# Splitting the MLP weights of a hybrid decoder layer by two loads

## Chip, cores and metric

The kernel runs on one core of one Trainium2 chip. The metric is the device time of one execution in microseconds (us). The engines are TensorE (PE), VectorE (DVE), ScalarE (ACT), GpSimd (POOL) and SyncE (SP); SP, ACT and POOL can issue loads and stores, which the DMA engines carry out.

## The reference

One layer of a decoder with 512 tokens and 1024 features in float32. After a mixing part (a linear recurrence beside an attention) the layer has an MLP, which is what the change touches:

```python
    D_FF = 4 * D_MODEL                      # 4096
    x = x + merged @ w_out[l]
    h2 = rmsnorm(x, norm_mlp_g[l])
    x = x + jnp.square(jax.nn.relu(h2 @ w_mlp_up[l])) @ w_mlp_down[l]
    h3 = rmsnorm(x, norm_ple_g[l])
    x = x + jax.nn.sigmoid(h3 @ w_ple_gate[l]) * (p[l] @ w_ple[l])
```

## The kernel before

Every matrix product is made in three passes. Each operand is split into a high part, rounded to the type float32r, and a low part, the rest; `prod` (L116) issues high by high, high by low and low by high for each slice of 128 rows of the contraction, all into one PSUM bank (L119, L120, L121). In the MLP's products the weights are the stationary operand, so that L119 and L120 use the weights' high part and L121 the low part.

The weights come from DRAM in "halves" of 128 partitions by 1024 elements, 512 KB each. `halves` (L70 to L101) lists all of them in the order of their use: those of the mixing part first, then for each of the two halves h of the 4096 hidden features 16 halves `up{h}_*`, for h = 0 two halves `ple`, and 16 halves `dn{h}_*`; last the gate `pg`. The MLP has 64 halves, 32 of up and 32 of dn. A half of the MLP gives PE 24 matmuls of 128x512.

`next_half` (L104) hands out the half that is ready and writes down the work for the next one: `w_half` (L63) has the raw tile loaded on SP's queue (`load_raw`, L46 to L49), and `split` (L51 to L53) makes the high part on ACT as a copy that rounds (L52) and the low part on DVE as raw minus high (L53). The pool `wp` (L39) has three buffers for each of the tags raw, whi and wlo, so a tile can be written again when the half three places earlier is done with it.

The order of the instructions on each engine is not written by hand: the tile framework places them when the kernel is built, by a reckoned time line, and puts in the waits. Each engine's queue, and the queue of loads on SP, ACT and POOL, is then worked off in that fixed order.

In the MLP (L540 to L586) each half of up goes into one PSUM bank of the pool pq (four banks), and ACT takes it out with Relu (L546) and Square (L547); `split` rounds it into the tile ah on ACT and puts the rest in al on DVE. Two halves of dn make one bank, which DVE multiplies by the row scale (L580) and adds to the residual (L581). In the second round the residual is also split for the next product (L583), squared and turned (L584 to L586). Between up and dn of the first round PE makes the small product ple (L554 to L568).

Of the kernel before, what the change touches and what calls it, by code (L numbers as in the profile page):

```python
# [11 lines left out]
AF = mybir.ActivationFunctionType  # L12
ALU = mybir.AluOpType
# [18 lines left out]
def hybrid_layer(ctx, tc, xT, pT, vecs, gfin, gates, w_in, w_bl, w_ba, w_out,  # L32
                 w_up, w_dn, w_pg, w_ple, out):
    nc = tc.nc
    sc, ve, pe, gp, sy = nc.scalar, nc.vector, nc.tensor, nc.gpsimd, nc.sync
# [6 lines left out]
    def f32(ap):  # L42
        return ap.bitcast(F32)


    def load_raw(src, name):  # L46
        raw = wp.tile([P, 1024], F32, tag="raw", name="raw_" + name)
        sy.dma_start(raw, src)
        return raw  # L49

    def split(hi, lo, src):  # L51
        sc.copy(hi, src)  # L52
        ve.tensor_tensor(lo, src, f32(hi), op=ALU.subtract)  # L53
# [5 lines left out]
    def w_tiles(name):  # L59
        return (wp.tile([P, 1024], F32R, tag="whi", name="whi_" + name),  # L60
                wp.tile([P, 1024], F32R, tag="wlo", name="wlo_" + name))

    def w_half(src, name, kt):  # L63
        raw = load_raw(src, name)
        hi, lo = w_tiles(name)
        split(hi, lo, raw)
        return tuple(t.rearrange("p (k n) -> p k n", k=kt) for t in (hi, lo))


# [34 lines left out]
    def next_half(name):  # L104
        n, cur = state["ready"]
        assert n == name, (n, name)
        state["i"] += 1
        if state["i"] < len(halves):
            c = halves[state["i"]]
            state["ready"] = (c[0], w_half(c[1], c[0], c[2]))  # L110
        return cur
# [615 lines left out]
```

## Time and profile before

| | us |
|---|---|
| median of 3 runs | 945.73 |
| lowest and highest | 943.81, 948.19 |
| profiled execution, whole | 946.11 |
| profiled execution, span of its trace | 944.0 |
| PE busy in the span | 929.5 |
| DVE busy | 542.4 |
| ACT busy | 471.3 |
| POOL busy | 67.9 |

The profile is of one execution. The span runs from its first to its last recorded instruction; 2.1 us of the execution lie around it. PE's matmuls are pipelined, and each shows some 0.39 us where the next one starts 0.23 us later; the pace is read from the starts. Where a group shows idle time, the name behind the arrow is what ended it. The granted clock is that of PE as a share of its full speed (2.4 GHz).

### The profile page before, as it was taken

What the parts mean: (1) busy time and instruction counts of PE and PEld (TensorE: products, weight loads), DVE (VectorE), ACT (ScalarE), POOL (GpSimd) and SP (SyncE); (2) the same over time, 40 slices, a digit from 0 to 9 for tenths busy, and PEclk for the clock granted to TensorE, in tenths of its full rate; (3) what the DMA queues carried; (4) which work ended last, traced back from release to release, by engine and by line L of the source; (5) the groups of instructions that cost most, each with busy time, mean ns of one, the idle gap of its engine ahead of it and who ended that gap; (6) DMA issues with size and microseconds to landing.
All of it is one profiled execution on the core that took longest, in us unless ns stands there. A gap on an engine that the chain in (4) does not pass through costs nothing.

```text
span 944.0 us, 12123 instructions
## 1 busy us (share of the span) xinstructions
PE 929.5 (98%) x4634; PEld 790.9 (84%) x4634; DVE 542.4 (57%) x818; ACT 471.3 (50%) x751; POOL 67.9 (7%) x147
## 2 busy tenths in 40 slices
PE   8999999999999999999999999999999999999996
PEld 7988888888888888888888888888888888888896
DVE  6796947688998986534655433333333333344476
ACT  6567676667776765412334444541214554333443
POOL 0010000133233332000000000000000000000000
PEclk9999999999999999999999999999999999999998
DMA  6241222211222222432232223323223223222312
GB/s 220 95 134 67 90 90 85 95 68 67 68 68 68 67 68 68 173 111 95 90 109 92 90 90 104 119 90 101 100 90 108 94 89 107 94 90 90 112 45 90
DMA packets 25401, 89.42 MB, mean 95 GB/s; under 512 B 2944, under 2 KB 3200, under 8 KB 25088
## 3 DMA queue, kind: packets, MB, share of 16 engines
q1 hardware_dynamic: 24768, 87.61, 27.5%
q10 hardware_dynamic: 576, 1.05, 0.3%
q8 instruction: 36, 0.59, 0.3%
q14 instruction: 21, 0.17, 0.1%
HBM read 86.55 MB, written 2.10 MB: 94 GB/s over the span
## 4 chain that ended last, share of the span: by engine, by line
PE 95%; ACT 2%; DVE 1%; DMA 1%; issue 1%; SPq 0%; ACTq 0%
PE ps_up L119 6%; PE dn L121 6%; PE ps_up L121 6%; PE dn L119 6%; PE dn L120 6%; PE ps_up L120 6%; PE t L445 2%; PE pgt L120 2%; PE pgt L121 2%; PE pgt L119 2%; PE ps_gl L121 2%; PE ps_k L121 2%; PE ps_q L119 2%; PE ps_ga L121 2%; PE ps_q L120 2%; PE ps_k L119 2%
## 5 line engine op out<-in xcount | busy, mean ns | idle before, releaser
L119 PE MATMUL dn<-ah,whi_dn 128*128 128x512 f32 x256 | 100.2, 391 | 0.0
L119 PE MATMUL ps_up<-h,whi_up 128*128 128x512 f32 x256 | 99.9, 390 | 0.0
L121 PE MATMUL ps_up<-h,wlo_up 128*128 128x512 f32 x256 | 99.7, 390 | 0.0
L121 PE MATMUL dn<-ah,wlo_dn 128*128 128x512 f32 x256 | 99.7, 389 | 0.0
L120 PE MATMUL ps_up<-h,whi_up 128*128 128x512 f32 x256 | 99.6, 389 | 0.0
L120 PE MATMUL dn<-al,whi_dn 128*128 128x512 f32 x256 | 99.6, 389 | 0.0
L52 ACT CAST whi_dn<-raw_dn 128x1024 fp32r<-128x1024 f32 x32 | 33.6, 1053 | 108.3 <-PE dn L120 82.9
L53 DVE TENSOR_TENSOR wlo_up<-raw_up,whi_up 128x1024 fp32r<-128x1024 f32 x32 | 39.2, 1224 | 73.4 <-ACT whi_up L52 73.4
L52 ACT CAST whi_up<-raw_up 128x1024 fp32r<-128x1024 f32 x32 | 33.7, 1054 | 91.3 <-PE ps_up L120 62.9
L53 DVE TENSOR_TENSOR wlo_dn<-raw_dn,whi_dn 128x1024 fp32r<-128x1024 f32 x32 | 39.0, 1222 | 67.6 <-ACT whi_dn L52 67.6
L432 DVE TENSOR_TENSOR_SCAN pr<-r,zero 128x128 f32<-128x128 f32 (+1 forms) x64 | 54.1, 845 | 10.7 <-POOL r L155 10.2
L121 PEld LDWEIGHTS dn<-ah,wlo_dn 128*128 128x128 f32 x256 | 48.1, 188 | 10.1
L121 PEld LDWEIGHTS ps_up<-h,wlo_up 128*128 128x128 f32 x256 | 48.1, 188 | 10.0
L120 PEld LDWEIGHTS ps_up<-h,whi_up 128*128 128x128 f32 x256 | 48.1, 188 | 10.0
L120 PEld LDWEIGHTS dn<-al,whi_dn 128*128 128x128 f32 x256 | 48.1, 188 | 9.8
L119 PEld LDWEIGHTS ps_up<-h,whi_up 128*128 128x128 f32 x256 | 48.1, 188 | 9.8
L119 PEld LDWEIGHTS dn<-ah,whi_dn 128*128 128x128 f32 x256 | 48.1, 188 | 9.7
L155 POOL TENSOR_SCALAR_AFFINE_SELECT r<-r 128x128 f32<-128x128 f32 x64 | 29.8, 466 | 192.6 <-ACT r L428 190.2
L428 ACT ACTIVATE r<-z 128x128 f32<-128x128 f32 (+1 forms) x64 | 28.5, 445 | 27.7 <-PE z L424 27.0
L580 DVE TENSOR_TENSOR d<-dn,sumsq 128x512 f32<-128x512 f32 x16 | 11.1, 692 | 52.1 <-PE dn L121 52.1
L155 POOL TENSOR_SCALAR_AFFINE_SELECT s<-s 128x128 f32<-128x128 f32 x64 | 33.6, 525 | 5.1 <-ACT s L430 3.3
L434 DVE TENSOR_TENSOR s<-s,pr 128x127 f32<-128x127 f32 (+1 forms) x64 | 31.8, 498 | 3.6
(282 smaller groups left out, 2424.0 us busy)
## 6 DMA issues: line engine op xcount, KB each, us to landing
raw_up<-in_w_up_dram SPq DMA_DIRECT2D x32, 512.0 KB, 3.4
raw_dn<-in_w_dn_dram SPq DMA_DIRECT2D x32, 512.0 KB, 3.5
raw_u<-in_w_in_dram SPq DMA_DIRECT2D x16, 512.0 KB, 3.6
raw_qk<-in_w_in_dram SPq DMA_DIRECT2D x16, 512.0 KB, 3.5
raw_gl<-in_w_in_dram SPq DMA_DIRECT2D x8, 512.0 KB, 3.4
raw_ga<-in_w_in_dram SPq DMA_DIRECT2D x8, 512.0 KB, 3.4
raw_bl<-in_w_bl_dram SPq DMA_DIRECT2D x8, 512.0 KB, 3.4
raw_ba<-in_w_ba_dram SPq DMA_DIRECT2D x8, 512.0 KB, 3.4
```

The lines of the kernel that those rows point to most:

```text
L52: sc.copy(hi, src)
L53: ve.tensor_tensor(lo, src, f32(hi), op=ALU.subtract)
L119: pe.matmul(ps, lh, rh, start=(first and i == 0), stop=False)
L120: pe.matmul(ps, lh, rl, start=False, stop=False)
L121: pe.matmul(ps, ll, rh, start=False, stop=(last and i == n - 1))
L155: gp.affine_select(block, block, pattern=[[-1, P]], compare_op=ALU.is_gt, fill=fill, base=0, channel_multiplier=1)
L428: sc.activation(r[:, 0:w], z[:, 0:w], AF.Sigmoid, scale=-0.125)
L432: ve.tensor_tensor_scan(pr[:, 0:w][:, ::-1], r[:, 0:w][:, ::-1], zero.broadcast_to([P, w]), 1.0, op0=ALU.mult, op1=ALU.add)
L434: ve.tensor_tensor(s[:, 0:w - 1], s[:, 0:w - 1], pr[:, 1:w], op=ALU.mult)
L445: turned[kbs[0]] = pe.transpose(pt[:, o:o + P], att[qb][:, kb * P:(kb + 1) * P], ident)
L580: ve.tensor_tensor(t, ps, rs2, op=ALU.mult)
```

## The change

For the halves of up and dn, the raw tile and `split` go away. A load issued on POOL's queue brings the weights straight into the high part's tile, whose type is float32r, so that the load converts. ACT writes the negated high part into the low part's tile. A second load of the same weights, also on POOL's queue, adds to what stands in that tile. All other halves stay as they were.

```diff
     def w_half(src, name, kt):
-        raw = load_raw(src, name)
         hi, lo = w_tiles(name)
-        split(hi, lo, raw)
+        if name.startswith(("up", "dn")):
+
+            gp.dma_start(hi, src)
+            sc.activation(lo, f32(hi), AF.Copy, scale=-1.0)
+            gp.dma_start(lo, src, accum_op=ALU.add)
+        else:
+            split(hi, lo, load_raw(src, name))
         return tuple(t.rearrange("p (k n) -> p k n", k=kt) for t in (hi, lo))
```

## Rows read from the trace of the kernel before

**Rows 1.** The page's first part: busy us, share of the span, instructions of each engine.
```profile
span 944.0 us, 12123 instructions
PE 929.5 (98%) x4634; PEld 790.9 (84%) x4634; DVE 542.4 (57%) x818; ACT 471.3 (50%) x751; POOL 67.9 (7%) x147
```

**Rows 2.** Windows after attention: length, busy us (instructions), granted clock, DMA share, GB/s.
```profile
core 0: us, PE busy (x) PEld busy (x) DVE busy (x) ACT busy (x) POOL busy (x), PEclk, DMA share, GB/s
384.00:438.00 54.00, 54.00 (x240) 44.74 (x239) 23.21 (x29) 16.31 (x21) 0.00 (x0) 1.00 0.39 137
438.00:523.00 85.00, 85.00 (x377) 70.41 (x376) 47.37 (x60) 28.79 (x37) 0.00 (x0) 1.00 0.29 98
523.40:893.00 369.60, 369.60 (x1674) 307.18 (x1673) 138.53 (x156) 148.23 (x201) 0.00 (x0) 1.00 0.29 99
893.00:944.00 51.00, 42.42 (x355) 42.21 (x353) 34.66 (x117) 21.21 (x56) 0.00 (x0) 0.95 0.18 63
```

**Rows 3.** Timeline of dn, first round: start us, us, instruction, [idle before, its end].
```profile
639.76 1.05 ACT L52 CAST whi_dn<-raw_dn 128x1024 fp32r<-128x1024 f32 x1 [4.38 <-PE dn L120]
639.79 0.39 PE L119 MATMUL dn<-ah,whi_dn 128*128 128x512 f32 x1
640.24 0.39 PE L121 MATMUL dn<-ah,wlo_dn 128*128 128x512 f32 x1
...
645.20 1.05 ACT L52 CAST whi_dn<-raw_dn 128x1024 fp32r<-128x1024 f32 x1 [4.38 <-PE dn L120]
...
650.64 1.05 ACT L52 CAST whi_dn<-raw_dn 128x1024 fp32r<-128x1024 f32 x1 [4.39 <-PE dn L120]
650.67 0.39 PE L119 MATMUL dn<-ah,whi_dn 128*128 128x512 f32 x1
651.12 0.39 PE L121 MATMUL dn<-ah,wlo_dn 128*128 128x512 f32 x1
```

**Rows 4.** Loads of up (512 KB) and L508 (two of 1024 KB): issue ns, landing.
```profile
L48 SPq DMA_DIRECT2D raw_up<-in_w_up_dram x32: 327/328/328, 498.7 to 767.2; - x32
DMA to landing us min/median/max: 3.0/3.4/4.0
...
L508 SPq DMA_DIRECT2D x<-in_xT_dram x2: 328/377/426, 391.8 to 392.2; - x2
DMA to landing us min/median/max: 5.0/6.0/7.1
```

**Rows 5.** Groups of instructions: busy us, mean ns of one, idle before.
```profile
L52 ACT CAST whi_dn<-raw_dn 128x1024 fp32r<-128x1024 f32 x32 | 33.6, 1053 | 108.3 <-PE dn L120 82.9 <-issue 15.1 <-PE ps_up L120 10.3
L53 DVE TENSOR_TENSOR wlo_up<-raw_up,whi_up 128x1024 fp32r<-128x1024 f32 x32 | 39.2, 1224 | 73.4 <-ACT whi_up L52 73.4
...
L155 POOL TENSOR_SCALAR_AFFINE_SELECT s<-s 128x128 f32<-128x128 f32 x64 | 33.6, 525 | 5.1 <-ACT s L430 3.3 <-PE t L445 0.4
L155 POOL TENSOR_SCALAR_AFFINE_SELECT r<-r 128x128 f32<-128x128 f32 x64 | 29.8, 466 | 192.6 <-ACT r L428 190.2 <-DVE wlo_qk L53 2.2
L301 POOL MEMSET gl<- 128x2048 f32 x1 | 1.8, 1831 | 0.0
```

**Rows 6.** Timeline of PE at the turn from ple to dn.
```profile
616.21 0.39 PE L120 MATMUL ple<-wlo_ple,psp 128*128 128x512 f32 x1
...
616.67 0.39 PE L119 MATMUL dn<-ah,whi_dn 128*128 128x512 f32 x1
...
617.12 0.39 PE L119 MATMUL ple<-whi_ple,psp 128*128 128x512 f32 x1
```

**Rows 7.** Windows at the start, columns as in the second group.
```profile
0.00:5.00 5.00, 3.80 (x18) 3.80 (x18) 0.00 (x0) 2.24 (x4) 1.88 (x9) 1.00 0.50 157
5.00:10.00 5.00, 4.03 (x26) 3.53 (x25) 2.87 (x5) 2.61 (x6) 0.00 (x0) 1.00 0.82 265
10.00:15.00 5.00, 2.85 (x17) 2.65 (x18) 4.51 (x8) 5.00 (x12) 0.00 (x0) 0.88 0.93 362
15.00:20.00 5.00, 5.00 (x36) 5.00 (x36) 5.00 (x10) 5.00 (x10) 0.00 (x0) 0.78 0.20 71
```

## The prediction

> **What bounds the kernel now.** I read the page's first two parts first: the matrix engine (PE) is busy for 98% of the span, ACT and DVE for about half of it [rows 1]. A mean over stages says nothing about one stage, so the windows come next. From 523.4 to 893 us, the two MLP products, PE is busy in all of 369.6 us at full granted clock, DVE for 138.5, ACT for 148.2, POOL for none, and the DMA engines are at 0.29 [rows 2]. So nothing that this change touches is late today: the MLP ends when PE has gone through its matmuls, and work taken from DVE is worth nothing there by itself. What matters is how far each weight tile is ahead of its use, and the timeline of two and a half weight halves shows that [rows 3]. ACT's rounding copies start at 639.76, 645.20 and 650.64, so a half (24 matmuls) takes PE 5.44 us. Each copy starts as soon as the half three places earlier is done (its idle time ends on PE, dn L120): the three buffers of whi and wlo are the gate. A tile whose copy starts at 639.76, while PE begins a half at 639.79, is used two halves later, at 650.67 (high part), and at 651.12 (low part, the third matmul). Its stationary load goes ahead by some 0.2 us. So **from the release of a buffer to the use of its low part there are about 11.1 us**, and today's chain, copy 1.05 and subtraction 1.22, takes 2.3 of them [rows 5], because the raw load was done long before in a buffer of its own: the SP queue's loads land in 3.4 us [rows 4].
>
> **The change, part by part.** Per half, 64 times, it removes a raw load on SP (0.33 us of SP) and a subtraction on DVE (1.22 us, 78 us in all) [rows 4, 5]. Both were hidden under PE: gain 0. ACT keeps one pass over 128x1024; the nearest row is the copy, 1.05 us [rows 5]. It now waits for a load instead of for a buffer, and Relu, Square and the rounding of the activations stand behind it on ACT; they are late by at most that wait, and four PSUM buffers stand between them and PE, so I cost that at nothing (if ACT fell over three halves behind, PE would pay it). The raw loads of ple, p and pg on SP now stand behind nothing of the MLP and come earlier: nothing, too. POOL's queue is empty from the end of attention on [rows 2], so the new loads stand behind each other alone.
>
> That is the cost. The load of the high part can't run ahead any more: it lands in whi, which PE frees only 11 us before use. The chain inside those 11.1 us becomes: load into whi, ACT's negation into wlo, accumulating load into wlo. And all 128 loads go through one in-order queue on POOL, where the second load of a half waits for ACT, and the next half's first load stands behind it.
>
> *Price of a load.* One 512 KB load lands after 3.4 us; of the two 1024 KB loads issued 0.4 us apart, the first lands after 5.0, the second after 7.1 [rows 4]. So 512 KB more is 1.6 us, with 1.8 us fixed, and a load that is issued behind another waits for that one's bytes (7.1 + 0.4 - 5.0 = 2.5 us for the second megabyte). The accumulating load reads the weights and the tile that it adds to. No row shows one. Below, it costs like one load (1.6 us of transfer); the nearest row above is twice the bytes (3.2 us), and I take that; an arithmetic path slower than the transfer would be more, and is a rival. The loads that round are taken as plain ones.
>
> By the Trainium skill (Collectives: The Full Stack, "The bandwidth ceiling: the fold count and why AG ≠ RS ≠ AR"), an add inside a DMA costs no arithmetic time but a second source read, and reduce-scatter came out at half of all-gather's rate for that. No row here shows it; it agrees with twice the bytes.
>
> *Price of an issue on POOL.* No row has one. Below stands SP's 0.33 us [rows 4], above POOL's longest instruction, a memset of 1.83 us [rows 5]. I take a surcharge of 0.5 us over an SP issue, near POOL's own 128x128 operation (0.47 to 0.53 us).
>
> The skill (DMA: Bandwidth & Descriptors, "Specifications") gives about 1 us to the first byte for loads issued from GpSimd and 0.6 for the others; by that the surcharge would be 0.4 and the forecast 6 us lower. No row here shows it.
>
> *Order A, each half in turn* (low of one half, then high of the next). From the issue of a low load, the next high load lands behind it after 1.8 + 3.2 + 1.6 = 6.6 us, ACT's pass and its hand-over add 1.15, then the next low load is issued: 7.75 us per half without surcharge. With a low load that costs one load: 1.8 + 3.2 + 1.15 = 6.15.
> *Order B, the next half's high load first.* At the release of a buffer the high load is issued and the waiting low load of the half before behind it. That low load lands after 6.6 us; PE needs it one period less the 5.44 us half plus 5.69 later (third matmul, less the stationary load), that is a period P + 0.25 after the release: P = 6.35. With a low load that costs one load: 5.0 us, hidden, and P stays 5.44.
>
> Which order stands is set by what is ready first when the kernel is built; that the order follows readiness and not the text, the trace shows where matmuls of dn stand amid those of ple [rows 6]. High load 3.4, ACT 1.15, surcharge 0.5 and some wait for ACT, together over 5.05, against a release every 5.44: nearly equal. I take B, with two reads and the surcharge: P = 6.85, 1.41 us more per half. With 62 of the 64 halves (the first two find POOL idle and free buffers) that is 87 us. The profiled execution took 946.1 us (span 944.0 and 2.1 around it) and the median is 945.7; 946.1 + 87 = **1033 us**, on either. PE would then be busy for 5.44 of 6.85 us, 79%. From 0 to 10 us it was busy for 76 and 81% at full granted clock; after 10 to 15 with 57% the clock stood at 0.88 and then 0.78 [rows 7]. So I count no loss of clock, but it is close.
>
> **The rivals.**
> 1. *Hidden, no slower.* Place: the low load in wlo. In order B it lands within 5.69 us of the release of the next buffer; that decides. It needs an add at the price of one load (5.0 us) and a surcharge under 0.7. For it: POOL, SP and DVE have nothing else to do there, and the DMA engines are at 0.29. Against: one of these bounds alone breaks it, and order A breaks it too. Time: 943.8 to 949. A real gain would need PE to have waited for DVE, and its 369.6 of 369.6 us leave no room; only the tail after 893 us could bring a few us.
> 2. *The add is slower than its bytes.* With transfer at four loads (6.4 us) order B lands the low load after 9.8 us, P = 9.8 + 0.5 - 0.25 = 10.05, 286 us more: 1232 us. PE would then be busy for about half of the time, like the stretch where the clock fell [rows 7], and part of that would come on top. For it: no row binds it from above. Against: two loads' worth is already counted.
> 3. *Order A with two reads*: 7.75 + 0.5 = 8.25, 174 us more: 1120 us; with one read 6.65, 75 us more: 1021 us.
> 4. *It does not do what it says*, and the load copies the bits without rounding, so that the low part is zero: the transfers and the waits stay the same, and so does the time.
>
> **How the numbers follow.** Forecast, with the one-read case of order A, 955 to 1085 us: 0.57. Order A with two reads, 1085 to 1160: 0.10. Slower than that by the add or the clock: 0.13. Hidden: 0.20, of which 0.03 for a gain over 0.5% (940.9 us or less) and 0.17 within 0.5%, which is about what a measurement of this kernel can tell from no change. The range, 943.8 to 1160, leaves out the slow add above and the gains below, 0.16 together.
>
> **What would show it.** Right: POOL's queue carries 128 loads; ACT's idle time before its pass over 128x1024 ends on a DMA and no longer on PE; PE has a gap before the first uses of wlo in each half, released by a DMA; ACT's passes in the dn stage are 6 to 8 us apart instead of 5.44. The time from issue to landing of the two kinds of load gives the disputed prices directly: one like the other speaks for one read, and the order of the issues on POOL tells A from B. Hidden: PE busy in all of the MLP windows. Wrong in size: low loads that land after 8 us or more, or a granted clock under 1.0 in the MLP.

## The result and the profile after

The changed kernel takes 1029.9 us (median; 1024.9 to 1032.8) against 946.8 before on the same chip: 83 us more, a ratio of 1.088 with a 95% interval of 1.084 to 1.092. The forecast was 1033. The profiled execution took 1024.9 us, so its trace shows 79 of the 83 us.

The page's first part (busy us, share of the span, instructions), its third part (queue, packets, MB, share of 16 DMA engines) and its sixth (us from issue to landing) after the change:

```profile
span 1023.2 us, 12172 instructions
PE 955.5 (93%) x4634; PEld 798.4 (78%) x4634; DVE 466.5 (46%) x754; ACT 472.3 (46%) x751; POOL 159.2 (16%) x275
...
q0 software_dynamic: 18432, 67.12, 28.8%
q1 hardware_dynamic: 15552, 54.05, 15.6%
...
whi_dn<-in_w_dn_dram POOLq DMA_DIRECT2D x32, 512.0 KB, 6.1
wlo_dn<-in_w_dn_dram POOLq DMA_DIRECT2D x32, 512.0 KB, 5.5
```

Against [rows 1], DVE lost 76 us of work and the span grew by 79. POOL's queue (q0) carries 128 loads of 512 KB; SP's queue carried 64 for the same halves before.

The window of the MLP after the change, and the last of its matmuls before and after (a tile's view: shortest, median and longest ns, first and last start in us):

```profile
523.40:967.00 443.60, 391.95 (x1630) 311.38 (x1629) 59.88 (x89) 144.59 (x194) 89.36 (x125) 0.96 0.67 154
```
```profile
L121 PE MATMUL dn<-ah,wlo_dn x256: 389/389/397, 618.5 to 887.2; 128*128 128x512 f32 x128
```
```profile
L126 PE MATMUL dn<-ah,wlo_dn x256: 387/389/796, 645.9 to 966.5; 128*128 128x512 f32 x128
```

All of the 79 us lie in the MLP: its first matmul starts at 523.6 us before and 523.3 after, its last at 887.2 and 966.5. Where PE was busy without a gap [rows 2], it is now idle for 51.6 us, and its matmuls fill some 28 us more, at a granted clock of 0.96. The clock is only a part of these 28: order B, below, has 0.99 and its matmuls still fill 24 us more. PE's idle time ends on the low parts, and the two lines of PE make 51.4 of the 51.6 us (view of the waits, PE and its weight loads: total, times, longest):

```profile
PEld dn L126 <- DMA wlo_dn<-in_w_dn_dram: 33.6, 17, 3.6
PEld ps_up L126 <- DMA wlo_up<-in_w_up_dram: 32.5, 19, 3.3
PE dn L126 <- DMA wlo_dn<-in_w_dn_dram: 27.0, 17, 3.2
PE ps_up L126 <- DMA wlo_up<-in_w_up_dram: 24.4, 15, 2.8
```

POOL's queue shows why they come late (timeline of POOL; L67 loads a high part, L69 adds into a low part; in brackets its idle time and what ended it):

```profile
680.02 0.86 POOL L69 DMA_DIRECT2D wlo_dn<-in_w_dn_dram  x1 [1.40 <-ACT wlo_dn L68]
680.57 0.87 POOL L67 DMA_DIRECT2D whi_dn<-in_w_dn_dram  x1
688.40 0.86 POOL L69 DMA_DIRECT2D wlo_dn<-in_w_dn_dram  x1 [6.96 <-ACT wlo_dn L68]
688.95 0.89 POOL L67 DMA_DIRECT2D whi_dn<-in_w_dn_dram  x1
693.59 0.55 POOL L67 DMA_DIRECT2D whi_dn<-in_w_dn_dram  x1 [3.75 <-PE dn L126]
696.49 0.88 POOL L69 DMA_DIRECT2D wlo_dn<-in_w_dn_dram  x1 [2.36 <-ACT wlo_dn L68]
699.07 0.86 POOL L69 DMA_DIRECT2D wlo_dn<-in_w_dn_dram  x1 [1.69 <-ACT wlo_dn L68]
699.62 0.88 POOL L67 DMA_DIRECT2D whi_dn<-in_w_dn_dram  x1
```

From 680.02 to 688.40 a low load, the next high load behind it, ACT's pass and the next low load follow each other: 8.4 us for one half, the prediction's order A. From 688.95 on two high loads stand ahead of two low loads. The builder, which places the instructions, mixed the two, and the mean is 5.44 + 83/62 = 6.78 us a half, counted over 62 halves as in the forecast.

### The profile page after: what moved, and what is told of

The parts are those of the page before. It is cut to its first block, busy times and chain, and to the rows that moved or that the text cites. A ratio compares the mean times of both kernels' runs of the same rounds, so it can differ in the third digit from the quotient of the medians.

```text
span 1023.2 us, 12172 instructions
## 1 busy us (share of the span) xinstructions
PE 955.5 (93%) x4634; PEld 798.4 (78%) x4634; DVE 466.5 (46%) x754; ACT 472.3 (46%) x751; POOL 159.2 (16%) x275
## 4 chain that ended last, share of the span: by engine, by line
PE 55%; issue 30%; POOL 8%; DMA 3%; ACT 2%; DVE 1%; SPq 0%; POOLq 0%; ACTq 0%
POOL whi_dn L67 2%; POOL whi_up L67 2%; POOL wlo_dn L69 2%; POOL wlo_up L69 2%; PE t L450 2%; PE pgt L124 2%; PE pgt L126 2%; PE pgt L125 2%; PE ps_gl L126 1%; PE ps_k L126 1%; PE ps_q L124 1%; PE ps_ga L126 1%; PE ps_k L124 1%; PE ps_q L125 1%; PE ps_q L126 1%
## 5 line engine op out<-in xcount | busy, mean ns | idle before, releaser
L126 PE MATMUL dn<-ah,wlo_dn 128*128 128x512 f32 x256 | 106.0, 417 | 27.0 <-DMA wlo_dn<-in_w_dn_dram 27.0
L124 PE MATMUL dn<-ah,whi_dn 128*128 128x512 f32 x256 | 104.4, 408 | 0.0
L125 PE MATMUL dn<-al,whi_dn 128*128 128x512 f32 x256 | 103.5, 404 | 0.0
L124 PE MATMUL ps_up<-h,whi_up 128*128 128x512 f32 x256 | 102.3, 400 | 0.0
L125 PE MATMUL ps_up<-h,whi_up 128*128 128x512 f32 x256 | 102.2, 399 | 0.0
L68 ACT ACTIVATE wlo_dn<-whi_dn 128x1024 fp32r<-128x1024 f32 x32 | 33.9, 1061 | 141.1 <-DMA whi_dn<-in_w_dn_dram 119.5
L53 DVE TENSOR_TENSOR al<-rl,ah 128x512 fp32r<-128x512 f32 x32 | 22.1, 692 | 167.0 <-ACT ah L52 167.0
L585 DVE TENSOR_TENSOR d<-dn,sumsq 128x512 f32<-128x512 f32 x16 | 11.1, 692 | 178.3 <-PE dn L126 178.3
L68 ACT ACTIVATE wlo_up<-whi_up 128x1024 fp32r<-128x1024 f32 x32 | 33.9, 1060 | 123.4 <-DMA whi_up<-in_w_up_dram 123.4
L67 POOL DMA_DIRECT2D whi_up<-in_w_up_dram x32 | 23.6, 738 | 181.2 <-PE ps_o L126 149.5
L69 POOL DMA_DIRECT2D wlo_up<-in_w_up_dram x32 | 27.8, 870 | 139.4 <-ACT wlo_up L68 139.4
L69 POOL DMA_DIRECT2D wlo_dn<-in_w_dn_dram x32 | 27.9, 873 | 124.0 <-ACT wlo_dn L68 115.8
```

The source lines that it names most:

```text
L67: gp.dma_start(hi, src)
L68: sc.activation(lo, f32(hi), AF.Copy, scale=-1.0)
L69: gp.dma_start(lo, src, accum_op=ALU.add)
L124: pe.matmul(ps, lh, rh, start=(first and i == 0), stop=False)
L125: pe.matmul(ps, lh, rl, start=False, stop=False)
L126: pe.matmul(ps, ll, rh, start=False, stop=(last and i == n - 1))
```

## The experiments

Theory Q is the prediction's: the two loads of a half wait for each other in POOL's in-order queue, with ACT between them, and three buffers leave 11.1 us from a buffer's release to the use of its low part. Rivals: one such load is enough by itself (S); the add is the whole cause (D); the buffers set the pace and the order on the queue does not (B). Differences are to the runs of the kernel before on the same chip.

**Each half of the change alone.** The high part by the converting load, the low part by DVE as before:

```diff
+            raw = load_raw(src, name)
             gp.dma_start(hi, src)
-            sc.activation(lo, f32(hi), AF.Copy, scale=-1.0)
-            gp.dma_start(lo, src, accum_op=ALU.add)
+            ve.tensor_tensor(lo, raw, f32(hi), op=ALU.subtract)
```

> One part alone: the high part comes by the converting load on POOL, the low part as before from a raw load on SP and DVE's subtraction. Theory Q (the two loads of a half wait for each other in POOL's in-order queue, with ACT between them, while three buffers leave 11.1 us): the chain is load 3.8 us, subtraction 1.22 and two hand-overs, some 5.3 of 11.1 us, so all is hidden: 943 to 950 us. Rival S (a load into a buffer that PE has just freed, issued by POOL, is enough to hold PE up): over 960 us.

Measured: 947.5 us, ratio 1.001 (0.9998 to 1.0021). S falls: a load into a buffer that PE has just freed costs nothing by itself that these runs can tell from no change. The other half, the adding load with the high part made by ACT from a raw load:

```diff
-            gp.dma_start(hi, src)
+            raw = load_raw(src, name)
+            sc.copy(hi, raw)
             sc.activation(lo, f32(hi), AF.Copy, scale=-1.0)
             gp.dma_start(lo, src, accum_op=ALU.add)
```

> The other part alone: raw load on SP and rounding copy on ACT as before, then ACT's negation and the accumulating load on POOL. Q: copy 1.05, negation 1.05, accumulating load 5.4 and hand-overs are about 8 of 11.1 us, so hidden: 943 to 955 us. Rival D (the adding load is what PE waits for, whatever stands beside it): 990 us or more.

Measured: 954.6 us, ratio 1.008 (1.007 to 1.010). D falls as the cause of the 83 us. The 8 us are a matter of one place, below. These two runs also price the loads, since q0 carries 64 loads of one kind in each (third part of the page, high part alone and low part alone):

```profile
q0 software_dynamic: 9216, 33.56, 12.0%
```
```profile
q0 software_dynamic: 9216, 33.56, 20.8%
```

12.0% of a span of 946.3 us over 64 loads is 1.77 us of all engines for a converting load; 20.8% of 951.4 is 3.09 for an adding one. Plain loads took 1.55 in the kernel before (27.5% of 944 us for 87.61 MB). The adding load costs two plain loads, as the prediction took it.

**The add alone taken away.** The second load writes over the negated high part instead of adding to it:

```diff
-            gp.dma_start(lo, src, accum_op=ALU.add)
+            gp.dma_start(lo, src)
```

> All as changed, in the same order on POOL, but the second load writes and does not add, so the low part holds the weights themselves (the sum of the products is another). This takes away the second read alone. Q: the low load and the high load behind it each land about 1.6 us earlier; a high load that waits in turn gives 6.6 us a half, the others 5.4, some 5.9 in the mean: 965 to 985 us. D (the add alone is the cause): 943 to 950. If an add costs no more than a plain load: 1025 to 1035, as changed.

Measured: 967.3 us, ratio 1.021 (1.019 to 1.023). All 128 loads stand in the same order on POOL as in the changed kernel, so the add is worth 62 us of the 83, and the queue with two loads that do not add still costs 21. With the second read a longer issue went away, too: a low load took POOL 0.53 us here and 0.87 with the add. How the 62 us divide between the two is not shown. Neither "the add alone" nor "the add is free" fits.

**The order on POOL's queue.** `tc.issue_after` holds an instruction behind another one of its engine. First every high load behind the low load of the half before (cut at ...):

```diff
+    last = {}
...
-            gp.dma_start(hi, src)
+            with ExitStack() as st:
+                if "lo" in last:
+                    st.enter_context(tc.issue_after(last["lo"].ins))
+                gp.dma_start(hi, src)
             sc.activation(lo, f32(hi), AF.Copy, scale=-1.0)
-            gp.dma_start(lo, src, accum_op=ALU.add)
+            last["lo"] = gp.dma_start(lo, src, accum_op=ALU.add)
```

> All as changed, but each high load is held behind the low load of the half before on POOL's queue, in all 64 halves. Q: 8.2 us a half, as the changed kernel shows where it does so, 2.76 more than 5.44, 62 times: 1105 to 1130 us. Rival B (the three buffers and the length of the chain alone set the pace, the order on the queue does not): 1020 to 1040.

Measured: 1119.4 us, ratio 1.181 (1.178 to 1.184), 173 us more, or 2.79 for each of 62 halves: 8.23 us a half. Its queue, by the timeline, and the landing of the high loads of dn:

```profile
707.99 0.86 POOL L74 DMA_DIRECT2D wlo_dn<-in_w_dn_dram  x1 [6.63 <-ACT wlo_dn L73]
708.54 0.88 POOL L72 DMA_DIRECT2D whi_dn<-in_w_dn_dram  x1
716.58 0.87 POOL L74 DMA_DIRECT2D wlo_dn<-in_w_dn_dram  x1 [7.16 <-ACT wlo_dn L73]
717.12 0.89 POOL L72 DMA_DIRECT2D whi_dn<-in_w_dn_dram  x1
724.81 0.87 POOL L74 DMA_DIRECT2D wlo_dn<-in_w_dn_dram  x1 [6.80 <-ACT wlo_dn L73]
```
```profile
DMA to landing us min/median/max: 3.8/6.3/6.8
```

Apart from 11 us at the turn around ple, none of its waits in the MLP ends on PE: the loop closes over POOL and ACT alone. The same order with a fourth buffer for the MLP's high and low parts is the sharpest test against B. The buffer comes from a small pool beside wp, which every fourth half uses (cut at ...):

```diff
+        wpool = wp
+        if name.startswith(("up", "dn")):
+            turn[0] += 1
+            if turn[0] % 4 >= 3:
+                wpool = extra["mw"]
-        hi, lo = w_tiles(name)
+        hi, lo = w_tiles(name, wpool)
...
+    extra["mw"] = ctx.enter_context(tc.tile_pool(name="mw", bufs=1))
```

> Each high load behind the low load of the half before, now with the fourth buffer. Q: the loop on POOL's queue (low load, high load behind it, ACT, next low load) takes 8.2 us a half and no buffer is in it: 1105 to 1130 us, as with three. Rival B (buffers set the pace): under 1080.

Measured: 1118.2 us, ratio 1.182 (1.180 to 1.184). A buffer more changes nothing. Then the other order, the next half's high load ahead of each low load (n2 and s2 are the next half's name and source; cut at ...):

```diff
+                nxt = gp.dma_start(early[n2][0], s2)
...
+                st.enter_context(tc.issue_after(nxt.ins))
             sc.activation(lo, f32(hi), AF.Copy, scale=-1.0)
             gp.dma_start(lo, src, accum_op=ALU.add)
```

> All as changed, but the high load of the next half is held ahead of each low load on POOL's queue throughout. Q: released buffer, high load, 0.55 us later the low load, which lands 6.6 us after its issue behind the high load; less 0.25 that is 6.9 us a half: 1020 to 1045 us. B (only buffers and the length of the chain count): as changed, 1020 to 1040, no difference from Q here.

Measured: 1039.5 us, ratio 1.100 (1.098 to 1.101), 93.7 us more, 6.95 a half with 62 of them. Here POOL waits for PE, that is for buffers (its timeline, and the landing of the low loads of up in the tile's view):

```profile
545.15 0.54 POOL L76 DMA_DIRECT2D whi_up<-in_w_up_dram  x1 [5.02 <-PE ps_up L138]
545.68 0.92 POOL L80 DMA_DIRECT2D wlo_up<-in_w_up_dram  x1
551.95 0.54 POOL L76 DMA_DIRECT2D whi_up<-in_w_up_dram  x1 [5.35 <-PE ps_up L138]
552.48 0.91 POOL L80 DMA_DIRECT2D wlo_up<-in_w_up_dram  x1
558.63 0.55 POOL L76 DMA_DIRECT2D whi_up<-in_w_up_dram  x1 [5.24 <-PE ps_up L138]
```
```profile
DMA to landing us min/median/max: 5.7/7.6/8.1
```

So this order should gain from the fourth buffer where the other did not; the same pool was added to it:

> As the kernel with the next high load always ahead of the low load, and a fourth buffer for the high and the low parts of the MLP's weights. Q: a low load has one half of 5.44 us more until its use, so it may land up to 11 us after its issue; hidden: 943 to 955 us. D (transfers of 2.3 us mean for each of two loads, or the add, limit the pace by themselves): 970 or more.

Measured: 957.1 us, ratio 1.013 (1.012 to 1.015), 82 us less than with three buffers. In most of the MLP PE is busy throughout, with the DMA engines at 0.89 (windows):

```profile
640.00:740.00 100.00, 100.00 (x443) 82.78 (x442) 12.45 (x18) 23.35 (x26) 26.63 (x38) 1.00 0.89 191
740.00:802.00 62.00, 62.00 (x275) 51.36 (x274) 8.31 (x12) 31.95 (x46) 16.06 (x23) 1.00 0.90 191
```

The traffic alone limits nothing here. The time is 2 us outside the expected range, and a part of it is lost at the place that cost the low part alone 8 us, as shown below. The pool without an order, as the builder then places the loads:

> As changed, with a fourth buffer alone; the order on POOL is left to the builder, which alternates single high and low loads with pairs of each. Q: the second high load of a pair no longer waits for a buffer, but where one low load stands ahead of the next high load 8.2 us go by: about 18 us for three halves, 6.0 a half: 970 to 1000 us. B (buffers alone): 943 to 955.

Measured: 1017.3 us, ratio 1.076 (1.074 to 1.079). That misses the expected range by 17 us. The buffer did what it was added for: high loads in the MLP wait for PE for 21 us in all, 84 in the changed kernel. But by the timeline of the whole MLP the steps from one low load to the next are still 8.4 us with one high load between them, and 8.9 and 2.4 in turn where two high loads stand ahead of two low ones (means of 25, 18 and 18 steps). Three halves take 19.7 us and not the 18 expected; why the pairs did not get shorter was not tried. What stands is that a buffer alone gives back 12 of the 83 us, and buffer and order together 72.

**The 8 to 11 us that were left.** Both kernels have one long stall of PE at the turn from ple to dn, 6.8 us in the low part alone and 6.7 with four buffers (low part alone: wait of PE, and the window):

```profile
PE dn L127 <- DMA wlo_dn<-in_w_dn_dram: 6.8, 1, 6.8
```
```profile
612.00:640.00 28.00, 21.16 (x87) 17.08 (x86) 0.69 (x1) 12.78 (x19) 3.46 (x4) 0.88 0.63 147
```

The loop over ple uses both of its weight halves to the end, so two of three buffers come free only there. The loops were exchanged, in the low part alone and in the kernel with four buffers:

```diff
-            for tb in range(NB):
-                t = slice(tb * P, (tb + 1) * P)
-                for hf in range(2):
+            for hf in range(2):
+                for tb in range(NB):
+                    t = slice(tb * P, (tb + 1) * P)
```

> The low part alone by the accumulating load, and the small product ple goes through its first weight half before its second, so that the first one's buffer is free 5.4 us earlier. The low part alone came out 8 us slower than before, and its trace has one stall of PE, 6.8 us at the turn from ple to dn, with the clock at 0.88 in that window. Theory P (that stall is all of the 8 us: both ple halves are held to the end of ple, and the next halves' chains start late): 944 to 949 us. Rival (the 8 us are spread over the 64 halves): 952 to 957.

> Next high load first, four buffers, and ple as in the run beside it. P: 944 to 950 us, the kernel before's time with twice its loads in the MLP. Rival (the rest of the 11 us is DMA traffic, at 0.87 to 0.90 in the MLP's windows): 954 to 959.

Measured: 949.6 us, ratio 1.004 (1.003 to 1.006), and 952.0, ratio 1.006 (1.004 to 1.007). Each is 5 us better than without the exchange, and the single wait is now 3.6 and 3.0 us long (the trace of the first is of an execution of 954.3 us, the longest of its twelve, so it shows what is left there and not the gain):

```profile
PE dn L127 <- DMA wlo_dn<-in_w_dn_dram: 3.6, 1, 3.6
```
```profile
PE dn L143 <- DMA wlo_dn<-in_w_dn_dram: 3.0, 1, 3.0
PE ps_up L143 <- DMA wlo_up<-in_w_up_dram: 1.8, 1, 1.8
```

So the place was right and the remedy half of one: the two lie 0.6 and 2 us above what theory P expected and below what its rivals expected, and what is left of PE's waits in the MLP is still one or two single ones, not a wait in each of 64 halves. What the last 4 and 6 us are was not tried further. No version beat the kernel before.

## Why the prediction held, point by point

**The bound and the hidden side.** PE had no gap to give back: 76 us of DVE work went away for nothing, as said. The chain behind the released buffer is what PE waits for, and POOL's queue is where it is slow. But PE waited before the low part in 32 halves of the 64 (17 and 15 in the waits above), and not in each, as my sign said. ACT's wait before its pass ended on PE in [rows 5] and now ends mostly on the high loads (group of instructions after, columns as there):

```profile
L68 ACT ACTIVATE wlo_dn<-whi_dn 128x1024 fp32r<-128x1024 f32 x32 | 33.9, 1061 | 141.1 <-DMA whi_dn<-in_w_dn_dram 119.5
```

**Prices.** The add: two loads taken, 3.09 against 1.55 us measured. The issue on POOL: 0.5 us over SP's 0.33 taken; 0.53 to 0.91 us in the medians measured, so 0.2 to 0.6 over. A high load behind a low one: landed 6.6 us after the low one's issue as taken, 6.8 as measured with order A (0.54 to its issue and 6.3 from there). A low load behind a high one: 6.6 and the surcharge of 0.5 after the high one's issue as taken, 0.53 + 7.6 = 8.1 as measured with order B, so 1 us short; that a converting load takes more transfer than a plain one (1.77 against 1.55 us) is a part of it. No row of before could show either. My sign that the landing of the two kinds of load gives the price of the add directly misled: in the changed kernel the adding loads land sooner, after 5.5 us, than the high loads, after 6.1. With one half of the change alone a high load landed after 4.6 to 4.7 us and an adding one after 5.5 to 6.1 (medians), so the landing shows also what stands ahead on the queue.

By the Trainium skill (Collectives: The Full Stack, "The bandwidth ceiling: the fold count and why AG ≠ RS ≠ AR") it is the second source read, and not the arithmetic, that makes reduce-scatter, which adds inside the DMA, half as fast as all-gather. The traces agree in size: 3.09 us is 2.0 times the plain load's 1.55, and 1.7 times the 1.77 of a load that converts as the adding one does. Which part of it is the read, no run separates.

**Order A** was put at 8.25 us a half, and 8.23 came out where it was forced. With one read it was put at 6.65; where the add alone was taken away, the steps with one high load between two low loads take 6.8 us on average.

**Order B** was put at 6.85 and came out at 6.95, but by two errors that cancel. The step that failed is "that is a period P + 0.25 after the release: P = 6.35": I let the low load land just in time and so gave all of its lateness to every half. In fact PE stops inside the half until the low part is there, and needs 5.19 us from then to the next release; from one release to the second next there are issue, landing and 5.19, so 2P = 0.5 + 6.6 + 5.2 and P = 6.15, 44 us more and not 87. With the measured 0.53 and 7.6 this gives 6.7, as in the lines of order B above (6.80 and 6.68 from one high load to the next), and near the mean of 6.95. The formula was too harsh and the landing too short. Rival 2's 10.05 us rests on the same step.

**Which order stands** was called nearly equal, and B was taken. The builder mixed them: 1.34 us a half more, below both A (2.79) and B (1.51). POOL's timeline over the whole MLP shows how the sum comes about, though no run forces this mixture. Of the 63 steps from one low load to the next, 24 have one high load in between, as in order A, and take 8.26 us on average. Another 38 come in pairs, one with two high loads in it (8.44) and one with none (2.94), 5.69 us a half; the last is the turn around ple. Over PE's 5.44 us that is 24 x 2.82 = 68 and 38 x 0.25 = 10 us, together 78 of the 79. So the halves in order A pay most of it, and the pairs, which the prediction did not have, are nearly free. That 1033 is close to 1029.9 is luck: mechanism, side and the bounds of the sum held, but its middle, 62 halves at 1.41 us each, is not how the time was lost. My sign for it, ACT's passes 6 to 8 us apart, was wrong in the same way: the low loads that follow them come at steps of 1.4 to 9.6 us, and 17.6 at the turn.

**The clock.** I counted no loss, from PE's busy share beside [rows 7], and named a clock under 1.0 as a sign of a wrong size. That sign came: the MLP's mean granted clock is 0.96, with PE busy for 88% of the window. The share did not tell the clock, as the same windows of order A and order B show:

```profile
523.40:1062.00 538.60, 427.49 (x1651) 330.35 (x1651) 59.66 (x88) 147.22 (x195) 89.36 (x125) 0.91 0.55 127
523.40:983.00 459.60, 388.02 (x1648) 304.07 (x1647) 61.45 (x91) 149.10 (x196) 90.28 (x125) 0.99 0.72 149
```

Order B has 0.99 with 84%. Order A has 0.91 with 79%, and its time still is POOL's loop of 8.2 us, so there the clock costs nothing; what it costs in the mixed order, where POOL waits for PE in places, no run separates.

**The rivals.** Nearly hidden was possible, with another buffer and the order B (957 and 952 us, above the rival's 949), but with three buffers in no order that was tried. A much slower add did not come. That the load might not round was not tried; the prediction gave it the same time, so the times cannot tell.

## What to carry to other kernels

Work that was taken from an engine off the path brought nothing here, and it can take a benefit with it: a raw tile of its own let the load run ahead, and loading straight into the operand's buffer put the load behind that buffer's release. Two dependent transfers of one step on one in-order queue cost a loop in every step (issue of the second, landing of the next step's first behind it, the engine between them), unless the next step's first transfer is issued ahead of this step's second. A fourth buffer was worth 82 us with that order, nothing with the other, and 12 us with the mixture. For a load that comes late by a fixed landing, write down the recurrence from release to release before summing: the lateness spreads over as many steps as there are releases in it.

## What the runs showed of the hardware

For 512 KB a load that adds into SBUF took 3.09 us of the 16 DMA engines (low part alone), a load that converts to float32r 1.77 (high part alone), a plain one 1.55 (kernel before). On POOL an adding load took 0.87 us to issue in the median, a load that does not add 0.53 (high part alone, and both loads where the add was taken away); right behind an adding load a high load took 0.88 as well (order A). With the DMA engines at 0.89 to 0.90, PE in the same windows stayed at its pace and at full granted clock (four buffers and order B).
